# Tiles of seven rows a partition in place of eight, in a kernel that streams through the DMA engines

## The chip, the cores and the metric

One core of one Trainium2 chip. The metric is the device time of one execution in microseconds (us); the profile's "span" is the part of it from the first to the last instruction, some 1.8 us shorter. In this text a "transfer" is one entry of the trace's DMA record: what one of the 16 DMA engines moves for one partition in one go. The record names the queue of a transfer and not its engine; I tell the engines apart by where one transfer starts as another ends. Across a standstill this match is uncertain by some 0.15 us. KB and MB in sizes and pitches are powers of two (64 KB is 65,536 bytes); GB/s are decimal.

## The reference

```python
batch, seq, dim = (32, 512, 2048)             # float32, 134 MB in, 67 MB out
x1, x2 = x[..., :1024], x[..., 1024:]
gelu_x1 = 0.5 * x1 * (1 + erf(x1 / np.sqrt(2)))
return gelu_x1 * x2
```

There are 16,384 rows of 8 KB, and each gives a row of 4 KB. Nothing is used twice.

## The kernel before

A tile is 1,024 rows, eight to a partition. The rows of one partition are neighbours in memory, so a partition's load is one run of 64 KB and its store one of 32 KB, and partition p + 1 starts 64 (32) KB after partition p.

```python
R, STEP = 8, 4
x_t = x_flat.rearrange("(n p r) d -> n p r d", p=P, r=R)
o_t = out_flat.rearrange("(n p r) d -> n p r d", p=P, r=R)
n_tiles = x_t.shape[0]                          # 16
...                                             # xpool, opool: two buffers each
def load(i):
    x_tile = xpool.tile([P, R, dim], x.dtype, name="x_tile")
    nc.sync.dma_start(out=x_tile, in_=x_t[i])
    return x_tile
def store(queue, i, o_tile, rows):
    queue.dma_start(out=o_t[i][:, rows, :], in_=o_tile[:, rows, :])

ahead = [load(0), load(1)]
for i in range(n_tiles):
    x_tile = ahead.pop(0)
    o_tile = opool.tile([P, R, half], out.dtype, name="o_tile")
    last = i == n_tiles - 1
    for r in range(0, R, STEP):
        rows = slice(r, r + STEP)
        nc.scalar.activation(...)               # GELU of the left half, in place
        nc.vector.tensor_mul(...)               # times the right half, into o_tile
        if last:
            store(nc.sync, i, o_tile, rows)
    if not last:
        store(nc.sync if i == n_tiles - 2 else nc.scalar, i, o_tile, slice(0, R))
    if i + 2 < n_tiles:
        ahead.append(load(i + 2))
```

Loads go out on SyncE's DMA queue and stores on ScalarE's, but for the last two tiles, whose stores are on SyncE's.

## Time and profile before

| | before |
|---|---|
| time, median of 3 runs | 471.43 us |
| span of the profiled run | 469.7 us |
| VectorE, ScalarE busy | 30%, 25% |
| DMA engines busy, all queues | 99.5% |
| rate from 44 to 449 us | 434 GB/s |
| a tile's period (load and store) | 29.0 us |
| computing a tile | 12.4 us |

The table says that the DMA engines set the time. Their transfers run from 1.74 to 468.5 us of the span; the prediction shows the lines this comes from.

### The profile page before, as it was taken

What the parts mean: (1) busy time and instruction counts of PE and PEld (TensorE: products, weight loads), DVE (VectorE), ACT (ScalarE), POOL (GpSimd) and SP (SyncE); (2) the same over time, 40 slices, a digit from 0 to 9 for tenths busy, and PEclk for the clock granted to TensorE, in tenths of its full rate; (3) what the DMA queues carried; (4) which work ended last, traced back from release to release, by engine and by line L of the source; (5) the groups of instructions that cost most, each with busy time, mean ns of one, the idle gap of its engine ahead of it and who ended that gap; (6) DMA issues with size and microseconds to landing.
All of it is one profiled execution on the core that took longest, in us unless ns stands there. A gap on an engine that the chain in (4) does not pass through costs nothing.

```text
span 469.7 us, 213 instructions
## 1 busy us (share of the span) xinstructions
DVE 140.2 (30%) x32; ACT 115.2 (25%) x33; POOL 0.2 (0%) x4
## 2 busy tenths in 40 slices
DVE  0070704307042070520606115060250702507043
ACT  1052306023060320603206041060500505005060
POOL 0000000000000000000000000000000000000000
DMA  8999999999999999999999999999999999999988
GB/s 357 446 446 357 446 446 446 402 446 458 391 446 444 433 463 402 435 413 491 402 419 430 491 402 402 446 491 402 402 446 480 413 402 444 449 446 402 474 375 357
DMA packets 4754, 201.35 MB, mean 429 GB/s; under 512 B 528, under 2 KB 528, under 8 KB 528
## 3 DMA queue, kind: packets, MB, share of 16 engines
q1 hardware_dynamic: 2736, 142.61, 70.5%
q10 hardware_dynamic: 2016, 58.72, 29.0%
q14 instruction: 2, 0.02, 0.0%
HBM read 134.22 MB, written 67.11 MB: 429 GB/s over the span
## 4 chain that ended last, share of the span: by engine, by line
DMA 77%; DVE 14%; ACT 6%; DVEq 1%; issue 0%; SPq 0%; ACTq 0%
DMA x_tile<-in_x_dram 77%; DVE o_tile L57 14%; ACT x_tile L54 6%; DVEq L93 1%; SPq L41 0%; ACTq L54 0%
## 5 line engine op out<-in xcount | busy, mean ns | idle before, releaser
L57 DVE TENSOR_TENSOR o_tile<-x_tile 128x4096 f32<-128x4096 f32 x32 | 140.2, 4422 | 321.6 <-ACT x_tile L54 321.6
L54 ACT ACTIVATE x_tile<-x_tile 128x4096 f32<-128x4096 f32 x32 | 114.0, 3608 | 340.5 <-DMA x_tile<-in_x_dram 340.5
L54 ACT ACT_TABLE_LOAD x1 | 1.3, 1283 | 0.7 <-PEq L82 0.7
L82 POOL MEMSET const-bfloat16-1.0<- 128x1 bf16 x1 | 0.1, 102 | 0.0
L82 POOL MEMSET const-uint8-127<- 128x1 uint8 x1 | 0.1, 101 | 0.0
L82 POOL MEMSET const-float32-0.0<- 128x1 f32 x1 | 0.1, 99 | 0.2 <-issue 0.2
L82 POOL MEMSET const-float32-1.0<- 128x1 f32 x1 | 0.1, 98 | 0.0
## 6 DMA issues: line engine op xcount, KB each, us to landing
out_dram<-o_tile ACTq DMA_DIRECT2D x14, 4096.0 KB, 41.8
out_dram<-o_tile SPq DMA_DIRECT2D x1, 4096.0 KB, 24.8
out_dram<-o_tile SPq DMA_DIRECT2D x2, 2048.0 KB, 6.9
x_tile<-in_x_dram SPq DMA_DIRECT2D x16, 45.5
```

Of the source, the lines that this page charges most:

```text
L54: nc.scalar.activation(out=x_tile[:, rows, :half], in_=x_tile[:, rows, :half], func=GELU)
L57: nc.vector.tensor_mul(out=o_tile[:, rows, :], in0=x_tile[:, rows, :half], in1=x_tile[:, rows, half:],)
L82: nc = _bacc.Bacc("TRN2", target_bir_lowering=False, num_devices=1)
L93: with _tile.TileContext(nc) as tc:
```

## The change

The idea: partitions 64 and 32 KB apart, both powers of two, might collide in memory; with seven rows to a partition they lie 56 and 28 KB apart. 128 rows a partition in all are 18 tiles of seven and one of two.

```diff
-    R, STEP = 8, 4
-    x_t = x_flat.rearrange("(n p r) d -> n p r d", p=P, r=R)
-    o_t = out_flat.rearrange("(n p r) d -> n p r d", p=P, r=R)
+    tiles, row = [], 0
+    while row < n_rows:
+        r = min(7, (n_rows - row) // P)
+        tiles.append((row, r))
+        row += r * P
...
+    def dram(flat, i):
+        row, r = tiles[i]
+        return flat[row : row + r * P].rearrange("(p r) d -> p r d", p=P)
...
-        nc.sync.dma_start(out=x_tile, in_=x_t[i])
+        nc.sync.dma_start(out=x_tile[:, :r, :], in_=dram(x_flat, i))
...
-        for r in range(0, R, STEP):
-            rows = slice(r, r + STEP)
+        for r in range(0, n, 4):
+            rows = slice(r, min(n, r + 4))
...
-            if last:
-                store(nc.sync, i, o_tile, rows)
-        if not last:
-            store(nc.sync if i == n_tiles - 2 else nc.scalar, i, o_tile, slice(0, R))
+        queue = nc.scalar if i < len(tiles) - 2 else nc.sync
+        queue.dma_start(out=dram(out_flat, i), in_=o_tile[:, :n, :])
```

(`n` is the number of rows that a partition has in tile i.) Besides the pitch and the size of the transfers, it changes two things at the end: the last tile is small, and its store is no longer cut in halves.

More of the change, by code (lines that the diff above doesn't have):

```diff
@@ L29 @@
     half = dim // 2
-    R, STEP = 8, 4
-    x_t = x_flat.rearrange("(n p r) d -> n p r d", p=P, r=R)
-    o_t = out_flat.rearrange("(n p r) d -> n p r d", p=P, r=R)
-    n_tiles = x_t.shape[0]
+    tiles, row = [], 0
[3 more added lines that the diff above has]
+        row += r * P
     xpool = ctx.enter_context(tc.tile_pool(name="xpool", bufs=2))
     opool = ctx.enter_context(tc.tile_pool(name="opool", bufs=2))
+    def dram(flat, i):
+        row, r = tiles[i]
+        return flat[row : row + r * P].rearrange("(p r) d -> p r d", p=P)
     def load(i):
-        x_tile = xpool.tile([P, R, dim], x.dtype, name="x_tile")
-        nc.sync.dma_start(out=x_tile, in_=x_t[i])
-        return x_tile
-    def store(queue, i, o_tile, rows):
-        queue.dma_start(out=o_t[i][:, rows, :], in_=o_tile[:, rows, :])
+        x_tile = xpool.tile([P, 7, dim], x.dtype, name="x_tile")
+        r = tiles[i][1]
+        nc.sync.dma_start(out=x_tile[:, :r, :], in_=dram(x_flat, i))
+        return x_tile
     ahead = [load(0), load(1)]
-    for i in range(n_tiles):
+    for i, (_, n) in enumerate(tiles):
         x_tile = ahead.pop(0)
-        o_tile = opool.tile([P, R, half], out.dtype, name="o_tile")
-        last = i == n_tiles - 1
-        for r in range(0, R, STEP):
-            rows = slice(r, r + STEP)
+        o_tile = opool.tile([P, 7, half], out.dtype, name="o_tile")
+        for r in range(0, n, 4):
+            rows = slice(r, min(n, r + 4))
             nc.scalar.activation(
@@ L61 @@
             )
-            if last:
-                store(nc.sync, i, o_tile, rows)
-        if not last:
-            store(nc.sync if i == n_tiles - 2 else nc.scalar, i, o_tile, slice(0, R))
-        if i + 2 < n_tiles:
+        queue = nc.scalar if i < len(tiles) - 2 else nc.sync
+        queue.dma_start(out=dram(out_flat, i), in_=o_tile[:, :n, :])
+        if i + 2 < len(tiles):
             ahead.append(load(i + 2))
```

## The prediction

> **What bounds the kernel now.** I first read the busy shares of the engines on the page, then its DMA rows.
>
> ```profile
> span 469.7 us, 213 instructions
> DVE 140.2 (30%) x32; ACT 115.2 (25%) x33; POOL 0.2 (0%) x4
> ...
> DMA  8999999999999999999999999999999999999988
> ...
> q1 hardware_dynamic: 2736, 142.61, 70.5%
> q10 hardware_dynamic: 2016, 58.72, 29.0%
> ```
>
> VectorE and ScalarE sleep 70 and 75% of the span. The 16 DMA engines are at 9 tenths or more in every slice but the first and the last two, and the two queues' packets take 70.5 + 29.0 = 99.5% of their time. To see whether "busy" also means "at full rate" I read a table of windows (columns: window, length, DVE, ACT, POOL busy, clock, DMA share, GB/s).
>
> ```profile
> 22.00:44.00 22.00, 8.76 (x2) 7.12 (x2) 0.00 (x0) 1.00 0.98 402
> 44.00:102.00 58.00, 17.52 (x4) 14.25 (x4) 0.00 (x0) 1.00 1.00 434
> 102.00:449.00 347.00, 105.13 (x24) 85.47 (x24) 0.00 (x0) 1.00 1.00 434
> 449.00:459.00 10.00, 5.98 (x2) 7.12 (x2) 0.00 (x0) 1.00 0.94 404
> ```
>
> From 44 to 449 us the rate is 434 GB/s. The trace's record of single transfers says why nothing is left there: a load of one partition (64 KB) takes 2.42 us in the 10th, the 50th and the 90th percentile alike, a store of one partition (32 KB) 1.21 us, a 16 KB store 0.61 us. Each engine moves one at a time, back to back. The difference of the first two, 32 KB in 1.205 us, is 27.2 GB/s an engine, 435 GB/s for 16; the rest is about 8 ns a transfer. Only two transfers of each engine are slow: the first of all (3.04 us on the engine that I followed, 0.62 too long) and one load at about 39 us (3.76 us, 1.34 too long), where the first store comes in. Last I read the start and the end, in the chain of waits in order of time (start, length, what) and in the timeline.
>
> ```profile
> 1.16 43.23 DMA x_tile<-in_x_dram
> 44.39 0.02 issue
> 44.41 3.62 ACT x_tile L54
> 48.04 0.02 issue
> 48.06 8.77 DVE o_tile L57 x2
> ...
> 405.29 44.00 DMA x_tile<-in_x_dram
> ```
>
> ```profile
> 434.51 27.63 SPq L45 DMA_DIRECT2D out_dram<-o_tile  x3
> 449.37 7.12 ACT L54 ACTIVATE x_tile<-x_tile 128x4096 f32<-128x4096 f32 x2 [20.18 <-DMA x_tile<-in_x_dram]
> 453.02 8.76 DVE L57 TENSOR_TENSOR o_tile<-x_tile 128x4096 f32<-128x4096 f32 x2 [18.54 <-ACT x_tile L54]
> ```
>
> The end is the part to look at, for there the queues can run dry. The store of tile 14 was issued at 434.5 us on the load queue, behind the last load (issued 405.29). By the single transfers it ran from 448.4 to 458.1 us, while the last tile was computed (449.4 to 461.8). The first half of the last store was issued at about 457.45 and began at 458.4. So the engines stood still for about 0.25 us; the last transfer ended at 468.2 to 468.5 us by engine, and the span at 469.73.
>
> **What the Trainium skill says.** "DMA: Bandwidth & Descriptors", section "Where 436 GB/s comes from", puts the ceiling at 435.2 GB/s; the 434 above agrees, so loads and stores together already run at it. The same page, section "Latency and other measured facts", row "HBM row pitch at large powers of two", tells of copies that lose rate at a pitch of 512 KiB and much more at MiB pitches, and of a few KiB of padding that cures it. That is the idea of this change; but the trace shows pitches of 64 and 32 KB at the ceiling, so this case has nothing to cure. The same page, section "Queues, rings and completion order", says that an engine takes turns between the queues that have work. The trace agrees, and shows the turn to be one partition's transfer: 2.42 us load, 1.21 us store, load, store, with two stores or two loads together at a tile's boundary. I lean on this most.
>
> **The change part by part.**
>
> *Bytes and compute.* The bytes are the same (134.2 MB read, 67.1 written). VectorE gets 18 instructions of 4 rows, 18 of 3 rows and one of 2 in place of 32 of 4 rows; all hidden but in the last two tiles.
>
> *Transfers.* Each engine handles 8 partitions of a DMA. Before: 8 x 16 loads, 8 x 15 stores of 32 KB, 8 x 2 of 16 KB, 264 in all. After: 19 loads and 19 stores, 304. Forty more at 8 ns is **+0.3 us**. By interpolation with 8 ns fixed: a 56 KB load is 2.11 us, a 28 KB store 1.06 us, a 16 KB load 0.61 us (as the 16 KB store), an 8 KB store 0.31 us.
>
> *Steady state.* Before, a tile is 8 loads and 8 stores, 29.00 us (the landings of tiles 1 and 3 lie 102.40 - 44.39 = 58.01 apart). After: 7/8 of it, 25.38, and 0.01 for the fixed part: 25.39 us. Computing a 7-row tile takes 3.61 (ScalarE, 4 rows) + 4.42 (VectorE, 4 rows) + 3.32 (3 rows, in proportion) + 0.1 = 11.45 us, far under the period.
>
> *Start.* First transfer at 1.74 us, as before. Load 0: 1.74 + 0.62 + 8 x 2.11 = 19.24; landing seen about 1.0 later, as before (21.68 to 22.64); computed at 20.2 + 11.45 = 31.7; there store 0 and load 2 are issued. Before, the store issued at 35.11 did not start until 42.43, after the transfer in progress and two more loads; those two were the last of load 1. After, the transfer in progress at 31.7 is load 1's sixth, so the store again starts when load 1 ends: 19.24 + 16.88 + 1.34 = 37.5 us. From then on the end of load i+1 is the start of store i, as it was (71.43 and 100.43, one period apart): the stores keep a backlog. The end of load 17 is 37.5 + 16 x 25.39 = 443.7 us.
>
> *End.* This is the only place that can cost. The old last tile was as large as all the others, and its load held the DMA engines while tile 14 was computed, and store 14 (4 MB) while tile 15 was. Now the last load is 2 rows. At 443.7 the work left for an engine is store 16 (8 x 1.06 = 8.5 us), load 18 (8 x 0.61 = 4.9 us), then stores 17 and 18. The first two, taking turns, end at 443.7 + 13.4 = **457.1**. Load 17's completion is seen some 1.9 us after its last byte while a store stands before it (71.43 to 73.49 before), at 445.6; tile 17 is computed at 457.05; its store is issued as one piece, and starts 1.0 us later (issue at 0.73, first transfer at 1.74): **458.05**. So there is a hole of about **0.95 us**, against 0.25 before: +0.7. Store 17 ends at 458.05 + 8.5 = 466.5. Tile 18 has landed by about 458, needs 1.8 + 2.2 us, and its store is issued by 462.5, in time to follow: + 8 x 0.31 = 469.0. Before, the span ended 1.5 us after this engine's last transfer (468.22 to 469.73); so 470.5. Measured time lay 1.70 above the span (471.43 - 469.73): 472.2. By sums instead: 471.43 + 0.3 + 0.7 = 472.4. I take **472.4 us**, +0.2%.
>
> **Rivals.**
>
> *The pitch mattered after all.* For it: the two slow transfers of an engine are loads. If both came from partitions that lie a power of two apart, and were cured, they give back 0.62 + 1.34 = 2.0 us: 470.4. More can't come, as the sum of transfers at their usual durations (8 x (16 x 2.413 + 15 x 1.21 + 2 x 0.61) = 463.9 us) and the fixed ends stay. Against it: they come once each, where a queue begins, not with any address that recurs.
>
> *A bigger hole at the end.* Its size is a difference of two moments 450 us into the run, and one unlucky turn moves it by a transfer (1.06 or 2.11 us). If the store backlog were smaller, or load 17 were seen later, it grows to 2 or 3 us: 474 to 475. For it: the first store waits behind transfers taken up ahead, and I do not know how their number depends on size. It can't be much worse: with no backlog at all the hole would be the 11.45 + 1.0 + 1.9 us of tile 17 less 4.9 us of load 18, some 9.5 us, and that would need the pattern of turns to be another one.
>
> *Transfers that do not stay whole.* If 56 KB a partition were cut in smaller pieces, say 8 KB, there would be some 1,536 transfers an engine in place of 264; 1,270 x 8 ns = 10 us: 482, slower by 2.2%. Against it: 64, 32 and 16 KB all went whole. The build shows the loads as 128x14336 and the stores as 128x7168 contiguous elements, the same form as before.
>
> **Range and chances.** The floor is the work of the DMA engines. To be 2% faster the kernel must end at 462 us, below the 463.9 us of transfers alone: 0.01, for a surprise in the ceiling. To be 2% slower it must lose 9.4 us, which takes the third rival or the extreme of the second: 0.03. The range takes the first rival's cure together with the extra hole at the low end (472.4 - 1.4 = 471.0) and a hole two or three us larger at the high end (475.2).
>
> **What would show the steps right or wrong.** In the changed profile: 434 GB/s between 40 and 440 us, neither more nor less; transfers of 2.11 and 1.06 us; landings of x_tile 25.4 us apart; load 17 ending near 444 us; in the tail a short time of low DMA share near 457 to 458 us, after which store 17 starts 1 us behind VectorE's last instruction on tile 17. If the first store starts before load 1 ends, or the turns are shared by bytes and not by transfers, the end is mis-sized. If a load takes longer than 2.2 us in the steady state, or is cut in pieces, the prediction is wrong at its base.

## The result, and the profile after

| | before | after |
|---|---|---|
| time, median of 6 runs each, same chip | 471.46 us | 472.47 us |
| lowest and highest | 471.22 to 471.88 | 472.40 to 473.19 |
| span of the profiled run | 469.7 us | 470.7 us |
| ratio after / before, 95% interval | | 1.0023 (1.0011 to 1.0036) |

A ratio is the mean time of one kernel's fast runs over that of the other's in the same rounds, so it is not quite the ratio of the medians. The changed kernel is about 1 us slower, clear of noise and far inside "the same at 2%". The page of the kernel after, in the rows that the prediction showed of before:

```profile
span 470.7 us, 242 instructions
## 1 busy us (share of the span) xinstructions
DVE 140.8 (30%) x37; ACT 116.0 (25%) x38; POOL 0.2 (0%) x4
...
DMA  9999999999999999999999999999999999999998
...
q1 hardware_dynamic: 3024, 138.94, 68.6%
q10 hardware_dynamic: 2448, 62.39, 30.7%
```

The picture is the same: 68.6 + 30.7 = 99.3% of the DMA engines' time in place of 99.5%. The missing 0.2% (0.9 us of the span, as far as one decimal can tell) is already most of the answer. A table of windows of the kernel after (window, length, DVE, ACT and POOL busy, clock, DMA share, GB/s) shows where it isn't:

```profile
65.40:440.00 374.60, 115.41 (x30) 93.75 (x30) 0.00 (x0) 1.00 1.00 433
...
456.00:459.00 3.00, 1.32 (x1) 0.78 (x1) 0.00 (x0) 1.00 0.65 279
```

For 375 us the rate is 433 GB/s; before it was 434. The pitch changed nothing there. Near 457 us the share drops to 0.65. (A short window is rough, because a transfer is counted where it starts; so I check it below with single transfers.) The timeline of the kernel after for the same place:

```profile
445.98 6.27 ACT L57 ACTIVATE x_tile<-x_tile 128x4096 f32<-128x4096 f32 x2 [19.08 <-DMA x_tile<-in_x_dram]
449.63 7.70 DVE L60 TENSOR_TENSOR o_tile<-x_tile 128x4096 f32<-128x4096 f32 x2 [17.65 <-ACT x_tile L57]
457.35 5.47 SPq L66 DMA_DIRECT2D out_dram<-o_tile  x2
458.22 1.91 ACT L57 ACTIVATE x_tile<-x_tile 128x2048 f32<-128x2048 f32 x1 [5.97 <-DMA x_tile<-in_x_dram]
460.16 2.29 DVE L60 TENSOR_TENSOR o_tile<-x_tile 128x2048 f32<-128x2048 f32 x1 [2.83 <-ACT x_tile L57]
```

VectorE ends tile 17 at 457.33 us, and only then, at 457.35, is its store issued. By then the DMA engines have nothing left: the single transfers of one engine of the kernel after (start in us, queue, size, duration in us) read

```
455.95  load  16 KB  0.61
456.56  load  16 KB  0.61     last of load 18, ends at 457.17
458.25  store 28 KB  1.06     first of store 17
459.32  store 28 KB  1.10
```

a hole of 1.08 us, give or take what the match across it leaves open. The same moment on all 16 engines, before and after:

| us, earliest to latest of the 16 engines | before | after |
|---|---|---|
| work ahead of the second-last (before: last) tile's store ends | 457.94 to 458.79 | 456.73 to 457.73 |
| that store starts | 458.31 to 458.79 | 458.20 to 458.34 |
| last transfer ends | 468.15 to 468.52 | 469.24 to 469.38 |

This table holds the point that is easily missed: the hole is not as long on all engines. The end is set by the engine that ends last. Before, the slowest engine had no hole at all (458.79 and 458.79); after, it lost between 458.20 - 457.73 = 0.47 and 458.34 - 457.73 = 0.61 us, while the fastest lost some 1.5 us that it had to spare anyway. The trace also shows where this comes from. The last transfer of load 17 ended between 443.39 and 444.39 us by engine, and ScalarE began at 445.98, 1.59 us after the last of them: the computing of tile 17, and with it store 17, waits for the slowest engine, while the fastest run ahead and then stand longest.

### The profile page after: what moved, and what is told of

It reads as the page before. It is cut to its first block, busy times and chain, and to the rows that moved or that the text cites. A ratio compares the mean times of both kernels' runs of the same rounds, so it can differ in the third digit from the quotient of the medians.

```text
span 470.7 us, 242 instructions
## 1 busy us (share of the span) xinstructions
DVE 140.8 (30%) x37; ACT 116.0 (25%) x38; POOL 0.2 (0%) x4
## 3 DMA queue, kind: packets, MB, share of 16 engines
q1 hardware_dynamic: 3024, 138.94, 68.6%
q10 hardware_dynamic: 2448, 62.39, 30.7%
## 4 chain that ended last, share of the span: by engine, by line
DMA 75%; DVE 15%; ACT 7%; issue 0%; ACTq 0%
DMA x_tile<-in_x_dram 75%; DVE o_tile L60 15%; ACT x_tile L57 7%; ACTq L57 0%
## 5 line engine op out<-in xcount | busy, mean ns | idle before, releaser
L60 DVE TENSOR_TENSOR o_tile<-x_tile 128x4096 f32<-128x4096 f32 (+2 forms) x37 | 140.8, 3845 | 321.7 <-ACT x_tile L57 321.7
L57 ACT ACTIVATE x_tile<-x_tile 128x4096 f32<-128x4096 f32 (+2 forms) x37 | 114.8, 3147 | 343.4 <-DMA x_tile<-in_x_dram 343.4
```

The lines of the kernel that those rows point to most:

```text
L57: nc.scalar.activation(out=x_tile[:, rows, :half], in_=x_tile[:, rows, :half], func=GELU)
L60: nc.vector.tensor_mul(out=o_tile[:, rows, :], in0=x_tile[:, rows, :half], in1=x_tile[:, rows, half:],)
```

## The experiments

The theory: the DMA engines ran at their ceiling before and after; the pitch is worth nothing; what is lost is lost in the hole, and a little in 40 more transfers an engine. The first rival: the loss is spread over the run. The second: the pitch gained something that the end took back.

### The hole taken away

The changed kernel, with the store of tile 17 in two pieces:

```diff
@@ inside the loop over r, after tensor_mul
+            if i == len(tiles) - 2:
+                nc.sync.dma_start(out=dram(out_flat, i)[:, rows, :], in_=o_tile[:, rows, :])
@@ after it
-        queue = ...; queue.dma_start(...)
+        if i != len(tiles) - 2:
+            queue = ...; queue.dma_start(...)
```

> The changed kernel with one edit: the store of tile 17 (the last tile of seven rows) goes out in two pieces, four rows as soon as they are multiplied, then three. Theory (the hole in the tail: the DMA engines stand still from 457.17 to 458.25 us, because store 17 waits for all of tile 17): the first piece is issued at about 454.1 us, while load 18 and store 16 still run until 457.2, so the hole vanishes; the time falls by about 1.0 us from 472.5 to 471.4 or 471.5, ratio to before 1.000. Rival (the 0.2% is the price of smaller transfers or of the pitch, spread over the run): the time stays at 472.4, ratio 1.002.

Measured: 471.86 us (5 runs, 471.85 to 472.00), ratio to before 1.0005 (0.9992 to 1.0017), before 471.59 us in this job. The timeline of this kernel shows the first piece going out at 454.19 us, three microseconds earlier than in the kernel after:

```profile
449.74 7.69 DVE L60 TENSOR_TENSOR o_tile<-x_tile 128x4096 f32<-128x4096 f32 x2 [17.66 <-ACT x_tile L57]
454.19 3.61 SPq L66 DMA_DIRECT2D out_dram<-o_tile  x2
```

By the single transfers no engine stands still there. None of its five runs was as slow as the fastest of the changed kernel (472.40), while before was no faster in this job; so, by the medians, the hole was most of the loss. (The changed kernel did not run again in this job, and the two intervals against before overlap; the trace, without the hole, agrees.) But the gain was 0.6 us, not the 1.0 expected. The last transfers say why: without the hole they end between 467.72 and 468.87 us by engine, a spread of 1.15; with it, between 469.24 and 469.38. The hole had brought the engines back in step, so that the slowest won 469.38 - 468.87 = 0.5 us by its removal. It is the same fact as in the table above, seen from the other side.

### The hole made larger

The changed kernel, with tile 17 computed in one piece, so that VectorE begins later:

```diff
-        for r in range(0, n, 4):
-            rows = slice(r, min(n, r + 4))
+        step = 7 if i == len(tiles) - 2 else 4
+        for r in range(0, n, step):
+            rows = slice(r, min(n, r + step))
```

> The changed kernel with the hole made larger: tile 17 is computed by one ScalarE and one VectorE instruction of seven rows instead of four and three. Nothing else moves. Theory (hole in the tail): VectorE ends tile 17 at about 445.9 + 6.3 + 7.7 = 459.9 instead of 457.3 us, store 17 starts 2.6 us later, and the time grows by those 2.6 us to about 475.1, ratio to before 1.0077. Rival (spread over the run): VectorE is off the path, 472.5, ratio 1.002.

Measured: 475.14 us, ratio 1.0078 (1.0064 to 1.0092), as expected. Windows of this kernel, with the columns as above:

```profile
456.00:458.00 2.00, 2.00 (x1) 0.00 (x0) 0.00 (x0) 1.00 0.52 221
458.00:460.00 2.00, 2.00 (x1) 1.59 (x1) 0.00 (x0) 1.00 0.00 0
460.00:462.00 2.00, 1.66 (x2) 0.32 (x1) 0.00 (x0) 1.00 0.77 330
```

Now no transfer starts between 458 and 460 us. Store 17 starts at 460.89 to 461.03 in place of 458.20 to 458.34, 2.7 us later, and the time grew by 475.14 - 472.47 = 2.7 us. VectorE, idle for 70% of the run, is on the path for this one tile.

### Only the pitch of the loads

The kernel before, with the loads 56 KB apart and all sizes and counts as they were. Neighbouring partitions overlap by a row, and the result is wrong:

```diff
-        nc.sync.dma_start(out=x_tile, in_=x_t[i])
+        block = x_flat[i * P * R : (i + 1) * P * R]
+        src = bass.AP(block.tensor, block.offset, [[7 * dim, P], [dim, R], [1, dim]])
+        nc.sync.dma_start(out=x_tile, in_=src)
```

> The kernel before with only the pitch of the loads changed: each partition still loads 64 KB, but partitions start 56 KB apart, so that neighbours overlap by one row and the result is wrong on purpose; sizes, number and order of all instructions and transfers are those of before. Theory (the DMA engines already run at the ceiling at a pitch of 64 KB): same time as before, 471.4 to 471.5, loads 2.42 us a partition. Rival (the pitch gained something in the changed kernel, and the tail took it back): up to 2 us faster, 469.5 to 470.9, with the two slow transfers of each engine (+0.62 and +1.34 us) gone or shorter.

Measured: 471.51 us, ratio 1.0004 (0.9990 to 1.0017). Loads took 2.418 us (median) as before, and each engine's two slow transfers were still there: on the engine that I followed the first took 3.10 us (3.04 before) and the one before the first store 3.71 us (3.76). The second rival falls for the loads: their pitch gained nothing that the end could take back. The stores' pitch was not tried alone; in the changed kernel a 28 KB store took 1.062 us, what interpolation between 16 and 32 KB gives, so it shows no gain either.

### The slow load before the first store

The kernel before, with the first row of each partition of tile 0 loaded through the queue that otherwise first works at 35 us:

```diff
+        first = 1 if i == 0 else 0
+        if first:
+            nc.scalar.dma_start(out=x_tile[:, :1, :], in_=x_t[i][:, :1, :])
-        nc.sync.dma_start(out=x_tile, in_=x_t[i])
+        nc.sync.dma_start(out=x_tile[:, first:, :], in_=x_t[i][:, first:, :])
```

> The kernel before, but the first row of each partition of tile 0 is loaded through ScalarE's DMA queue instead of SyncE's, so that this queue is used from the start and not first at 35 us. Theory A (the slow transfer of +1.34 us at about 39 us is the first use of a second queue): it vanishes there and is hidden in the start, the time falls by about 1 us to 470.4. Theory B (it is the turn from reading to writing, or anything else that comes with the first store): it stays at about 39 us, the time is that of before plus the 8 extra transfers of each engine, 471.5.

Measured: 471.45 us, ratio 0.9996 (0.9984 to 1.0009). Each engine still had one load near 39 us that was too long, by 0.94 us on average over the engines in place of 1.08. So the first use of the queue is not the cause. The slow load is on every engine the last before the first store; but load 2 is issued at the same moment as that store (35.1 us), and no run parts the two. Which of them it comes from, and why, stays open.

### What a transfer costs by itself

The kernel before, with the eight rows of a partition 128 rows apart, so that every row is a transfer of its own:

```diff
-    x_t = x_flat.rearrange("(n p r) d -> n p r d", p=P, r=R)
-    o_t = out_flat.rearrange("(n p r) d -> n p r d", p=P, r=R)
+    x_t = x_flat.rearrange("(n r p) d -> n p r d", p=P, r=R)
+    o_t = out_flat.rearrange("(n r p) d -> n p r d", p=P, r=R)
```

> The kernel before, but the eight rows of a partition lie 128 rows apart in memory, so that each load is cut into transfers of 8 KB and each store into 4 KB: 2,048 transfers an engine instead of 264, bytes and instructions the same. Asks what a transfer costs by itself, the term of 40 extra transfers in the prediction. Theory (8 ns each): 1,784 x 8 ns = 14 us, time about 485.7; transfers of 0.31 and 0.16 us. Rival (the fixed part is hidden when many follow each other): about 472.

Measured: 479.10 us, ratio 1.0160 (1.0145 to 1.0175). That is 479.10 - 471.51 = 7.6 us for 1,784 more transfers an engine, 4.3 ns each. It is not lost at the start or the end: a tile's period in the middle of the run, with 112 more transfers an engine, grew from 29.00 to 29.53 us, some 4.7 ns each. Both were off: the price is real, but half of what I took. My 8 ns came from durations (2 x 1.213 - 2.418 us), and in the record a transfer starts some 5 ns before the one ahead of it ends; from start to start, loads of 64 KB lay 2.41 us apart. The Trainium skill ("DMA: Bandwidth & Descriptors", section "Why small descriptors are slow (HBM only)") gives a fixed overhead of about three cycles a packet. Whether the 4.3 ns are that overhead no run here shows; this run also moved the partitions to a pitch of 8 KB, so not all of it need be a price of the transfer.

### A pitch that does matter

Is the change's idea wrong, or was there only nothing to cure? The kernel before, with the same sizes, but each partition owning 128 neighbouring rows: loads 1 MB apart, stores 512 KB.

```diff
-    x_t = x_flat.rearrange("(n p r) d -> n p r d", p=P, r=R)
-    o_t = out_flat.rearrange("(n p r) d -> n p r d", p=P, r=R)
+    x_t = x_flat.rearrange("(p n r) d -> n p r d", p=P, r=R)
+    o_t = out_flat.rearrange("(p n r) d -> n p r d", p=P, r=R)
```

> The kernel before with the same transfers of 64 and 32 KB, but each partition owns 128 neighbouring rows, so that partitions lie 1 MB apart for loads and 512 KB for stores, both powers of two; result correct. Asks whether a power-of-two pitch costs anything at all in this kernel. Theory (each transfer is long and contiguous, the DMA engines are at their ceiling whatever the pitch): 471.5, loads 2.42 us and stores 1.21 us. Rival (partitions a large power of two apart collide in memory, [...]and the change aimed at the right thing at the wrong pitch): loads or stores longer by 3% or more, time 485 us or more.

Measured: 483.58 us, ratio 1.0254 (1.0237 to 1.0271). My theory's 471.5 was wrong here. Windows of this kernel:

```profile
2.00:44.00 42.00, 8.76 (x2) 7.13 (x3) 0.00 (x0) 1.00 1.00 376
44.00:102.00 58.00, 17.52 (x4) 14.25 (x4) 0.00 (x0) 1.00 1.00 415
102.00:449.00 347.00, 105.13 (x24) 85.46 (x24) 0.00 (x0) 1.00 1.00 432
```

and the same windows of the kernel before:

```profile
2.00:44.00 42.00, 8.76 (x2) 7.13 (x3) 0.00 (x0) 1.00 0.98 409
44.00:102.00 58.00, 17.52 (x4) 14.25 (x4) 0.00 (x0) 1.00 1.00 434
102.00:449.00 347.00, 105.13 (x24) 85.47 (x24) 0.00 (x0) 1.00 1.00 434
```

The DMA engines are as busy as ever (share 1.00), yet they move 376 GB/s and not 409 in the first stretch: here the transfers themselves became longer, and a busy share alone would not have told it. After the first load, more than half of the loads up to 100 us took over 2.5 us (before: 3%), later only 4%; the longest took 4.24 us, and not the 3.6 that I wrote into the expectation of the next run. The loss is mostly at the start, when all engines begin at once; that they then drift apart and so stop colliding is my reading, and was not tested. What the kernel pays is the lateness of the slowest engine: its last load ended at 461.26 us, before at 448.88, 12.4 us later, and the time grew by 12.1.

Next, the loads of that kernel 127 rows (1,016 KB) apart instead of 128, the result again wrong:

```diff
-        nc.sync.dma_start(out=x_tile, in_=x_t[i])
+        rows_at = x_flat[i * R : n_rows]
+        src = bass.AP(rows_at.tensor, rows_at.offset, [[127 * dim, P], [dim, R], [1, dim]])
+        nc.sync.dma_start(out=x_tile, in_=src)
```

> The kernel with partitions 1 MB apart (e5, 483.6 us, loads up to 3.6 us in the first 90 us), but its loads start 127 rows (1,016 KB) apart instead of 128 (1 MB); they overlap and the result is wrong on purpose; stores stay 512 KB apart; sizes, number and order of transfers are the same. Theory (what slowed e5 is that its load pitch is a large power of two, and a pitch 8 KB off it cures that): loads of 2.42 us from the second on, time about 471.5. Rival (it is the distance itself, whatever the number): about 483.6 again, with slow loads in the first 90 us.

Measured: 474.75 us, ratio 1.0065 (1.0047 to 1.0083); 8.8 us of the 12.1 are gone. The windows of this kernel:

```profile
2.00:44.00 42.00, 8.76 (x2) 7.13 (x3) 0.00 (x0) 1.00 0.97 408
44.00:102.00 58.00, 17.52 (x4) 14.25 (x4) 0.00 (x0) 1.00 1.00 429
```

The first stretch is back at 408 GB/s; so it was the exact pitch of 1 MB, and not the distance of about a megabyte as such, that slowed the loads. One other pitch was tried; that it has to be a power of two is not shown. But 3.2 us remained that I had not expected. To see whose they are, the loads of the kernel before (64 KB apart) with only its stores 512 KB apart, the result wrong:

```diff
-    o_t = out_flat.rearrange("(n p r) d -> n p r d", p=P, r=R)
+    o_t = out_flat.rearrange("(p n r) d -> n p r d", p=P, r=R)
```

> The kernel before with its loads as they are (64 KB apart) and only its stores 512 KB apart; rows land in other places, so the result is wrong on purpose. Asks where the 3.2 us come from that remained when the loads were moved off 1 MB (e7, 474.75 us). Theory (from the stores' pitch of 512 KB, which was left): 474 to 475 us, the slowest engine's last load ends near 451 us. Rival (from loads 1,016 KB apart, which is still not as good as 64 KB): 471.5, last load ends near 448.9 us, and then most of e5's 12 us are of the loads alone.

Measured: 474.65 us, ratio 1.0054 (1.0032 to 1.0075), the time of the kernel with loads 1,016 KB apart. The slowest engine's last load ended at 453.08 us in the profiled run, 2 us later than I had set for it. So the remainder goes with the stores' pitch of 512 KB: stores some 3 us and, by subtraction, loads some 9. It is the loads, though, that mostly show it: after each engine's first load, 73 loads were over 3% too long (before: 18), and 23 stores (before: 1). Moving the loads' pitch 8 KB off 1 MB was a sound remedy here, though the stores at 512 KB were given none; at 64 and 32 KB there was no illness.

## Why the prediction was right

The time (472.4 us predicted, 472.47 measured) and the direction, a loss of a fifth of a per cent, were right. By its steps, on the engine that it followed:

| step | predicted | in the trace after |
|---|---|---|
| a 56 KB load, a 28 KB store (us) | 2.11, 1.06 | 2.116, 1.062 |
| load 0 ends | 19.24 | 19.39 |
| first store starts, when load 1 ends | 37.5 | 37.33 |
| period | 25.39 | 25.39 (37.33, 62.72, 88.10) |
| load 17 ends | 443.7 | 443.83 |
| store 16 and load 18 end | 457.1 | 457.17 |
| load 17 seen by ScalarE | 445.6 | 445.98 |
| tile 17 computed | 457.05 | 457.33 |
| store 17 starts | 458.05 | 458.25 |
| hole on this engine | 0.95 | 1.08 |
| last transfer ends | 469.0 | 469.27 |
| span | 470.5 | 470.7 |

*The ceiling.* Right: 433 GB/s after, 434 before; moving the loads alone to a 56 KB pitch gave 471.51 us.

*The turns.* Right: load, store, load, store, with two of a kind at a tile's boundary. At the end the small loads of the last tile alternated with the 28 KB stores of tile 16, so that store 16 kept the engines busy until 457.17 us; had the turns been shared by bytes, the moments at the end would have been others.

*The hole.* The mechanism is right, shown by the run that removed it (471.86 us) and the run that enlarged it (475.14). Its size on the path was off: I took the difference on one engine, 0.95 - 0.25 = +0.7 us. The end is set by the slowest engine, which lost about 0.5 us after and nothing before. The moment of store 17 was set 0.2 us too early, and the largest term behind that is a reading: ScalarE was to see load 17 some 1.9 us after its last byte, where the figures quoted for it (71.43 to 73.49) give 2.06; after, it was 2.15 on this engine.

*The 40 transfers.* I took 8 ns each, +0.3 us; the run with 1,784 more found 4.3 ns, so +0.17 us. Together the two terms make about 0.7 us of the 1.0 measured. The last transfer ended 469.38 - 468.52 = 0.86 us later in the profiled runs, so some 0.2 us is not assigned; it is within what the runs of one kernel differ by (471.22 to 471.88), and I leave it open. Both of my terms were too large, by some 0.3 us together, and the sum hit because about as much has no cause assigned to it. That is luck. (Two smaller things: the slow load before the first store was sized by the 1.34 us of one engine, the largest of the 16, whose mean is 1.08; and the 463.9 us of transfers alone come to 463.8.)

*The rivals.* The cure by the pitch fell. The larger hole did not come by itself. Transfers stayed whole: 56 KB went in one piece.

## What to carry to other kernels

When transfers run back to back at one fixed duration, and bytes over time match the ceiling, as here, a better address pattern has little to give; look at whether "busy" hides long transfers before changing a pitch. Where the DMA engines are the bound, time is lost only where they stand still or their transfers lengthen: so the last load must be long enough to cover the computing of the tile before it, or that tile's store must go out in pieces. And a hole costs what the slowest of the 16 engines loses by it, not the mean.

## What the Trainium skill lacked or had wrong

- "DMA: Bandwidth & Descriptors", section "Latency and other measured facts", row on the row pitch, starts at 512 KiB and tells of copies between HBM tensors. It lacks loads into SBUF and smaller pitches: here 64 KB (loads) and 32 KB (stores) cost nothing (471.5 us, 434 GB/s); 1 MB and 512 KB together cost 12.1 us, most of it in the first 100 us (376 GB/s up to 44 us, 432 after 102); 1,016 KB for the loads took 8.8 us of that back. Its remedy, a few KiB of padding, agrees, though here the pitch was made 8 KB shorter.
- The same page, section "Queues, rings and completion order", has an engine drain a packet of typically 9 to 17 descriptors before it turns to the next queue. Here a turn was a single transfer, whether of 64 and 32 KB or of 8 and 4 KB: load, store, load, store in the record of single transfers (if an entry of that record is one descriptor, which no run here shows).
- The same page, section "Latency and other measured facts", gives a first byte after about 600 ns for DMAs issued from SyncE. Here the first transfer started 1.0 us after the issue (0.73 to 1.74 us), and store 17 of the changed kernel 0.9 us after (457.35 to 458.25); whether the record's start of a transfer is the page's first byte is not shown.
- No page that I read has the 1.1 us (mean over the engines) by which one load of every engine was too long just before the first store, from near 39 us before and 34 us after; using the store queue earlier did not take it away (0.94 us).
